# Turning the pairs' results by DMA instead of on TensorE in a two-layer macaron trunk

## The chip, the cores and the metric

The kernel runs on one core of one Trainium2 chip. The metric is the device time of one execution in microseconds (us); lower is better. The kernel before the change takes 1689.77 us, the median of three runs (1689.21 to 1690.2).

## The reference

Two layers work on a residual stream `x` of 512 tokens by 1024 features in float32. The parts that this case is about are the feed-forward networks (FFNs), two in a layer, four in all:

```
for l in range(DEPTH):                      # DEPTH = 2
    x = x + 0.5 * swiglu(rms_norm(x, ffn1_norm[l]), ffn1_wg[l], ffn1_wu[l], ffn1_wd[l])
    h = rms_norm(x, mix_norm[l])
    z = h @ w_in[l]                         # q, k, v and the three parts of a short convolution
    ...                                     # attention over a window of 128, and the convolution
    x = x + concat([attn_out, conv_out]) @ w_out[l]
    x = x + 0.5 * swiglu(rms_norm(x, ffn2_norm[l]), ffn2_wg[l], ffn2_wu[l], ffn2_wd[l])
return rms_norm(x, final_norm)

def swiglu(h, w_gate, w_up, w_down):
    return (silu(h @ w_gate) * (h @ w_up)) @ w_down     # 1024 -> 2816 -> 1024
```

## The kernel before

**Products.** Each float32 operand is split into a rounded high part and a low part, and a product is three matmuls: high by high, low by high, high by low. A weight tile is 128 partitions by 1024 elements (512 KB). SP loads it into one of eight `raw` buffers (line 188), ScalarE casts the high part into `wh` (line 204), VectorE subtracts to get `wl` (line 205), and there are three buffers of each. `take_split` hands out the next tile and asks for the split of the tile two further on (`SPLIT_AHEAD = 2`), which in turn asks for the load of a unit four further on (`LOAD_AHEAD = 4`). The order of the weight tiles is written down beforehand by `plan()` (line 376), in the same order in which the stages use them.

**Stages of an FFN.** The 2816 inner columns are 11 blocks of 256. The tuples `FIRST`, `INNER` and `LAST` (lines 32 to 40) list the stages: `p` is a plain block, `w` a pair of blocks taken together, `u` a single block, `s` a down-projection shared by two pairs, `d` a plain down-projection of the listed blocks. The first FFN of the kernel is `FIRST`, the two in the middle are `INNER`, the last one `LAST`. There are four pairs in the first FFN and five in each of the other three, 19 in all.

**A pair** is done by `winograd2` (line 1024): a seven-product scheme (`Seven`, `CHAINS`) in place of eight. Its seven steps run `stream` (line 832) twice each, 12 matmuls of 128x512 a time, so 24 matmuls a step. The results lie with tokens on the partitions. The next product needs inner columns on the partitions, so the four token blocks `ups[0..3]` of a pair have to be turned: 512 tokens by 512 columns. `turn(c)` does that with four TensorE transposes of 128x128 (line 1078) into PSUM and a ScalarE copy into `raws` (line 1082), or, for the pair of blocks 9 and 10, a split straight from PSUM. The four `turn`s of a pair wait in a list, `pending`, and are taken from it by `turns(step)` in steps 0, 1 and 2 of the next pair (one, one and two of them), or by `flush` in the second shared stage.

**Down-projection.** `share` (line 849) uses the seven-product scheme again, on two pairs at once: forms of the turned results are made by `Seven.make`, and VectorE adds the products to the stream (line 872). `down` (line 332) does the plain blocks: for each half `o` of the 1024 output columns, four PSUM banks, one for each token block; VectorE adds each to the stream (line 1150). In `INNER` and `LAST` the last stage is `("d", (0, 9, 10))`, block 0 waiting from the beginning of the FFN. In its second half (`o = 1`) three tiles are held and the first two token blocks are finished before the other two, so that the next norm can begin; `norm.pull()` puts the norm's transposes between products. In `LAST` that stage is run by `Finale` (line 1161), which also does the last norm and the stores.

**Buffers.** Turned operands, the norm's seven forms and their sums share eight buffers, tag `xf` (line 124); gates, `ups` and other 128x512 pieces share fourteen, tag `g2`; whole turned pairs (`raws`) use four, tag `g8`.

**Order.** The program is written in one order for all engines; a scheduler then sets the order on each engine by readiness and by place in the program, except in regions under `manual_schedule`, where the written order stands. Each engine and each DMA queue takes its instructions in order. SP's queue has the weight loads, POOL's queue the accumulating loads that make weight sums (line 199).

Of the kernel before, what the change touches and what calls it, by code (L numbers as in the profile page):

```python
# [10 lines left out]
BF16 = mybir.dt.bfloat16  # L11
I32 = mybir.dt.int32
AF = mybir.ActivationFunctionType
ALU = mybir.AluOpType

P = 128
D = 1024
S = 512
# [54 lines left out]
def trunk_kernel(  # L73
# [139 lines left out]
    def need_split(g):  # L213
        while state["split"] <= min(g, len(order) - 1):
            n = state["split"]
            u, what = order[n]
            far = what == "far"
            if what in (None, "wide", "far"):
                need_raw(u if far else u + LOAD_AHEAD)
# [111 lines left out]

    def down(acts, blocks, norm=None):

        last = len(blocks) - 1

        def products(acc, t, i, wh, wl):
            tok = slice(t * P, (t + 1) * P)
            ah, al = acts[blocks[i]]
            for k in range(2):
                for n, (a, w) in enumerate(((ah, wh), (al, wh), (ah, wl))):  # L340
                    nc.tensor.matmul(  # L341
                        acc,
                        a[:, k, tok],
                        w[:, k, :],
                        start=i + k + n == 0,
                        stop=i == last and k == 1 and n == 2,
                    )

        for o in range(2):
            accs = [psum("mm", [P, S], f"down_{state['group']}_{t}") for t in range(NT)]  # L350
            if o and norm:
                by_hand()
            if o and last:
                held = [take_split(SPLIT_AHEAD - i)[1:] for i in range(last + 1)]
                ahead = state["group"]
                for t in range(2):
                    for i, w in enumerate(held):
                        products(accs[t], t, i, *w)
                    yield t, o, accs[t]
                for i, w in enumerate(held):  # L360
                    for t in range(2, NT):
                        products(accs[t], t, i, *w)
                        if i == last:
                            yield t, o, accs[t]
                        if norm and i + 1 == last:
                            norm.pull()
                    need_split(ahead + i)
                continue
            for i in range(last + 1):
                _, wh, wl = take_split()  # L370
                for t in range(NT):
                    products(accs[t], t, i, wh, wl)
                    if i == last:
                        yield t, o, accs[t]

    def plan():
# [25 lines left out]
        def ffn(wg, wu, wd, stages):  # L402
            for what, b in stages:
# [13 lines left out]
                if what != "d":  # L417
                    continue
                for half in range(2):
                    for k in b:  # L420
                        u = add_unit((wd, 2 * k, 2, half * S, S))
                        if half == 0 or stages is not LAST:
                            order.append((u, "wide"))

# [461 lines left out]
    def ffn(norm, stages, whole, after=None, late=None):  # L886
# [137 lines left out]
        def winograd2(b, between=None):  # L1024
# [5 lines left out]
            ups = [None] * NT  # L1030
            kept = {}

            def keep(what, u, src):
# [3 lines left out]
            for step, (acc, operand, start) in enumerate(CHAINS):  # L1037
# [5 lines left out]
                for h in range(2):  # L1043
                    _, wh, wl = take_split()
                    stream(accs[acc], wh, wl, xh, xl, h, start)
                    for u in range(2):
# [15 lines left out]
                        if step == 5:  # L1062
                            ups[u] = kept["u2", u]
                            nc.vector.tensor_sub(ups[u], out, ups[u])
                            nc.vector.tensor_mul(ups[u], ups[u], gates[u])
                        if step == 6:
                            nc.scalar.activation(gates[2 + u], out, AF.Silu)
                            nc.vector.tensor_mul(ups[2 + u], ups[2 + u], gates[2 + u])
                turns(step)
                if between:  # L1070
                    between(step)
            if b in blocks:
                raws[b] = g8(f"raw_a_{name}", F32, (P, KC // 2, S))

            def turn(c, tag="sc"):
                tp = psum(tag, [P, S], f"at_{name}_{c}")
                for t in range(NT):
                    nc.tensor.transpose(  # L1078
                        tp[:, t * P : (t + 1) * P], ups[t][:, c * P : (c + 1) * P], ident
                    )  # L1080
                if b in raws:
                    nc.scalar.copy(raws[b][:, c, :], tp)
                    return
                if b + c // 2 not in acts:
                    acts[b + c // 2] = both(f"a_{name}_{c}", shape=(P, 2, 2, S))
                hi, lo = acts[b + c // 2]
                split(hi[:, c % 2, :], lo[:, c % 2, :], tp)

            pending.extend(lambda *tag, c=c: turn(c, *tag) for c in range(NT))

# [3 lines left out]
        def turns(step):  # L1094

            if step < 2:
                flush()
            if step == 2:
                flush(2, "mm")
# [4 lines left out]
        pending = []  # L1104

        def flush(n=1, *tag):
            for _ in range(n):
                if pending:
                    pending.pop(0)(*tag)

        for i, (what, b) in enumerate(stages):
# [11 lines left out]
            if what == "s" and b == sevens[0]:  # L1123
                then = shared(sevens[1])
                sums = ("t3", "t2") if stages[-1] == ("s", sevens[1]) else ("t2", "t3")
                share(
                    ops, 0.5, ahead(then, {3: ("b11",), 4: ("b21",), 5: sums[:1], 6: sums[1:]})
                )
            elif what == "s":
                share(  # L1130
                    then,
                    0.5,
                    None if first else lambda step: 2 <= step < 6 and flush(1, "aux"),
                    after=after if final else None,
                )
# [6 lines left out]
            if final and not after:  # L1142
# [3 lines left out]
                return  # L1146
            for n, (t, o, acc) in enumerate(down(acts, b, after if final else None)):
                if b == (0,) and first:
                    norm.make(*{0: ("t3",), 4: ("t1",)}.get(n, ()))
                nc.vector.scalar_tensor_tensor(  # L1150
                    xt(t, o), acc, 0.5, xt(t, o), op0=ALU.mult, op1=ALU.add
                )
                flush()
# [356 lines left out]
```

## Time and profile before

| | us |
|---|---|
| median of three runs | 1689.77 |
| lowest and highest | 1689.21, 1690.2 |
| the profiled execution | 1689.48 |
| its span, first to last instruction | 1687.7 |

| engine | busy us | share of the span |
|---|---|---|
| PE (TensorE matmuls) | 1674.4 | 99% |
| DVE (VectorE) | 1324.7 | 78% |
| ACT (ScalarE) | 953.4 | 56% |
| POOL (GpSimd) | 182.3 | 11% |

The mean granted TensorE clock is 0.999. The core moves 279.85 MB by DMA, 166 GB/s over the span. In the rows, names are those of tiles without their numbers: `wh` and `wl` are the high and low part of a weight tile, `x`, `y`, `w` the accumulators of a pair, `x_s`, `y_s`, `w_s` those of a shared down-projection, `at` the PSUM bank into which a pair's result is turned, `raw_a` its copy, `down` the plain down-projection. `SPq` is SP's DMA queue. An arrow after an idle time names what ended it.

### The profile page before, as it was taken

The page shows a single profiled execution, that of the slowest core. Times are in us where ns is not written, and L with a number is a line of the kernel's source. Part 1 is how long each engine was busy: PE and PEld are TensorE (multiplying, and loading weights), DVE is VectorE, ACT ScalarE, POOL GpSimd, SP SyncE. Part 2 cuts the span into 40 slices and gives each one's busy share as a digit, 9 for nine tenths or more (in the row PEclk, how much of TensorE's full clock was granted, in tenths as well). Part 3 has the DMA queues.
Part 4 walks back from the last instruction along what each step waited for, and adds up shares of the span by engine and source line. Part 5 has one row for each costly group of instructions (what it writes and reads, how often), then busy time and mean ns, then how long its engine had stood idle before and what let it go on. Part 6 is the DMA issues. An engine that isn't in the chain of part 4 may idle for free.

```text
span 1687.7 us, 21919 instructions
## 1 busy us (share of the span) xinstructions
PE 1674.4 (99%) x8222; PEld 1408.9 (83%) x8222; DVE 1324.7 (78%) x1734; ACT 953.4 (56%) x1361; POOL 182.3 (11%) x164
## 2 busy tenths in 40 slices
PE   9999999999999999999999999999999999999998
PEld 7888898888889888888898888888988898888887
DVE  7987679867799666899596668995587986678993
ACT  6445555556566555655365556554565765556553
POOL 0011111000110111111001111110001101111101
PEclk9999999999999999999999999999999999999999
DMA  8367778721495777788547776883225947777871
GB/s 250 99 176 194 184 196 209 194 72 51 125 226 124 195 181 185 187 224 214 136 100 188 187 186 176 229 219 105 59 63 151 221 119 185 188 185 185 226 188 50
DMA packets 189310, 279.85 MB, mean 166 GB/s; under 512 B 8948, under 2 KB 73492, under 8 KB 189204
## 3 DMA queue, kind: packets, MB, share of 16 engines
q1 hardware_dynamic: 150900, 203.34, 38.2%
q0 software_dynamic: 37600, 74.46, 26.1%
q8 instruction: 64, 1.05, 0.2%
q10 hardware_dynamic: 704, 0.66, 0.1%
q14 instruction: 42, 0.34, 0.1%
HBM read 263.74 MB, written 2.10 MB: 158 GB/s over the span
## 4 chain that ended last, share of the span: by engine, by line
PE 92%; DVE 6%; ACT 1%; issue 1%; DMA 0%; SPq 0%; DVEq 0%; ACTq 0%
PE x L838 25%; PE y L838 12%; PE x_s L838 10%; PE w L838 6%; PE down L341 5%; PE y_s L838 5%; PE acc L291 4%; PE acc L292 4%; PE acc L294 4%; PE w_s L838 3%; PE acc L318 2%; PE at L1078 2%; DVE wl L205 2%; PE x_m L838 1%; PE up L953 1%; PE acc L736 1%
## 5 line engine op out<-in xcount | busy, mean ns | idle before, releaser
L204 ACT CAST wh<-raw 128x1024 fp32r<-128x1024 f32 (+1 forms) x494 | 516.4, 1046 | 555.8 <-PE x L838 128.1
L205 DVE TENSOR_TENSOR wl<-raw,wh 128x1024 fp32r<-128x1024 f32 (+1 forms) x494 | 598.7, 1214 | 243.7 <-ACT wh L204 241.3
L838 PE MATMUL x<-wh,ft 128*128 128x512 f32 x608 | 188.7, 391 | 0.0
L838 PE MATMUL y<-wh,ft 128*128 128x512 f32 x608 | 188.4, 391 | 0.0
L838 PE MATMUL x<-wh,fb 128*128 128x512 f32 x608 | 187.2, 389 | 0.0
L838 PEld LDWEIGHTS x<-wh,fb 128*128 128x128 f32 x608 | 113.9, 188 | 23.5
L838 PEld LDWEIGHTS x<-wh,ft 128*128 128x128 f32 x608 | 113.1, 188 | 22.8
L838 PEld LDWEIGHTS y<-wh,ft 128*128 128x128 f32 x608 | 113.1, 188 | 22.7
L838 PE MATMUL x<-wl,ft 128*128 128x512 f32 x304 | 118.3, 389 | 0.0
L838 PE MATMUL y<-wl,ft 128*128 128x512 f32 x304 | 118.3, 389 | 0.0
L838 PE MATMUL x<-wl,fb 128*128 128x512 f32 x304 | 118.3, 389 | 0.0
L199 POOL DMA_DIRECT2D raw<-in_ffn_wu_dram x39 | 47.2, 1213 | 529.3 <-DMA raw<-in_ffn_wu_dram 272.5
L838 PE MATMUL w<-wh,fb 128*128 128x512 f32 x304 | 95.2, 394 | 0.0
L291 PE MATMUL acc<-hh,wh 128*128 128x512 f32 x240 | 94.6, 394 | 0.0
L294 PE MATMUL acc<-hh,wl 128*128 128x512 f32 x240 | 94.0, 391 | 0.0
L292 PE MATMUL acc<-hl,wh 128*128 128x512 f32 x240 | 93.6, 390 | 0.0
L341 PE MATMUL down<-wh,a 128*128 128x512 f32 x288 | 89.4, 392 | 0.0
L838 PE MATMUL y_s<-wh,ft_s 128*128 128x512 f32 x256 | 79.5, 392 | 0.0
L838 PE MATMUL x_s<-wh,ft_s 128*128 128x512 f32 x256 | 79.1, 390 | 0.0
L199 POOL DMA_DIRECT2D raw<-in_ffn_wg_dram x39 | 47.0, 1205 | 265.1 <-DMA raw<-in_ffn_wu_dram 102.0
L838 PE MATMUL x_s<-wh,fb_s 128*128 128x512 f32 x240 | 74.2, 390 | 0.0
L231 DVE TENSOR_TENSOR raw<-raw,raw 128x1024 f32<-128x1024 f32 x58 | 70.8, 1220 | 0.6
(320 smaller groups left out, 3429.1 us busy)
## 6 DMA issues: line engine op xcount, KB each, us to landing
raw<-in_ffn_wu_dram SPq DMA_DIRECT2D x126, 512.0 KB, 3.6
raw<-in_ffn_wd_dram SPq DMA_DIRECT2D x104, 512.0 KB, 4.8
raw<-in_ffn_wg_dram SPq DMA_DIRECT2D x86, 512.0 KB, 4.7
raw<-in_ffn_wu_dram POOLq DMA_DIRECT2D x39, 512.0 KB, 6.7
raw<-in_ffn_wg_dram POOLq DMA_DIRECT2D x39, 512.0 KB, 6.1
raw<-in_w_in_dram SPq DMA_DIRECT2D x36, 512.0 KB, 3.8
raw<-in_ffn_wd_dram POOLq DMA_DIRECT2D x32, 512.0 KB, 7.5
raw<-raw POOLq DMA_DIRECT2D x20, 512.0 KB, 6.6
```

Of the source, the lines that this page charges most:

```text
L199: nc.gpsimd.dma_start(out=r, in_=rows_of(*more), accum_op=ALU.add)
L204: nc.scalar.copy(hi, raw)
L205: eng.tensor_sub(lo, raw, f32(hi))
L231: nc.vector.tensor_add(a11, a11, s1)
L291: nc.tensor.matmul(acc, hi[:, k, :], rhs[k][0], start=k == first, stop=False)
L292: nc.tensor.matmul(acc, hi[:, k, :], rhs[k][1], start=False, stop=False)
L294: nc.tensor.matmul(acc, lo[:, k, :], rhs[k][0], start=False, stop=k == last)
L318: nc.tensor.matmul(accs[j][:, t * H : (t + 1) * H], w[:, k, :], x_, start=t + k + i == 0, stop=k == KC - 1 and i == 2, skip_group_check=True,)
L341: nc.tensor.matmul(acc, a[:, k, tok], w[:, k, :], start=i + k + n == 0, stop=i == last and k == 1 and n == 2,)
L736: nc.tensor.matmul(opening[n], (lo if part == "w" else hi)[:, k, :], xl if part == "x" else xh, start=n not in begun, stop=k == KC - 1 and ...
L838: nc.tensor.matmul(accs[u], x_[:, 2 * h + k, tok], w[:, k, :], start=start and h + k + i == 0, stop=h + k == 2 and i == 2, skip_group_chec ...
L1078: nc.tensor.transpose(tp[:, t * P : (t + 1) * P], ups[t][:, c * P : (c + 1) * P], ident)
```

## The change

Four things are changed.

1. `turn` goes. `apart(t)` reads each token block of a pair's result as pairs of 16-bit halves and lets ScalarE copy the low halves to one plane and the high halves to another (two copies of 128x512). `send(t)` issues one DMA transpose on SP's queue for the block's two planes, 128 partitions by 1024 halves, into its place in a tile `pt` of tag `xf`. `join(n)` lets ScalarE put the halves of two 128-column pieces together again (two copies of 128x1024) in the room of `raws`, and, for the pair of blocks 9 and 10, splits them from there.
2. When this happens is a table of steps: token blocks 0 and 1 are sent after step 0 of the next stage, 2 and 3 after step 1, and the pieces joined after steps 5 and 6. The first shared stage calls `turns` too; the second no longer does.
3. In `INNER` and `LAST`, block 0's down-projection is a stage of its own behind the first pair, so that the last `d` has blocks 9 and 10 only.
4. For the last `d` with a norm behind it there is `down_end`: all four weight tiles (two blocks by two halves) are held at once, one of them in an `xf` buffer (`"room"` in the order), and token blocks 0 and 1 are finished for both halves before 2 and 3 begin.

```diff
 INNER = (
-    ("p", 0), ("w", 1), ("w", 3), ("w", 5), ("w", 7), ("w", 9), ("s", 1), ("s", 5),
-    ("d", (0, 9, 10)),
+    ("p", 0), ("w", 1), ("d", (0,)), ("w", 3), ("w", 5), ("w", 7), ("w", 9), ("s", 1), ("s", 5),
+    ("d", (9, 10)),
 )
-LAST = INNER[:-1] + (("d", (0, 9, 10)),)
+LAST = INNER[:-1] + (("d", (9, 10)),)
...
-            hi = wpool.tile(shape, F32R, tag="wh", bufs=3, name=f"wh_{n}")
-            lo = wpool.tile(shape, F32R, tag="wl", bufs=3, name=f"wl_{n}")
+            if what == "room":
+                hi, lo = both(f"wx_{n}", shape=(P, 2, 2, S))
+            else:
+                hi = wpool.tile(shape, F32R, tag="wh", bufs=3, name=f"wh_{n}")
+                lo = wpool.tile(shape, F32R, tag="wl", bufs=3, name=f"wl_{n}")
...
+    def down_end(acts, blocks, norm):
+        a, b = blocks
+        held = []
+        def tile_of(n):
+            while len(held) <= n:
+                held.append(take_split(max(0, min(SPLIT_AHEAD, 3 - len(held))))[1:])
+            return held[n]
...
+        by_hand()
+        for t in range(2):
+            for o in range(2):
+                acc = bank(t, o)
+                for i in range(2):
+                    products(acc, t, 2 * o + i)
+                yield t, o, acc
+        ahead = state["group"]
+        for o in range(2):
+            accs = {t: bank(t, o) for t in (2, 3)}
+            for i in range(2):
+                n = 2 * o + i
+                for t in (2, 3):
+                    products(accs[t], t, n)
+                    if i:
+                        yield t, o, accs[t]
+                if n in (1, 2):
+                    norm.pull()
+                if n:
+                    need_split(ahead + n - 1)
...
+            def apart(t):
+                planes.append(g2(f"pl_{name}_{t}", U16, (P, 2, S)))
+                src = ups[t].bitcast(U16).rearrange("p (n z) -> p z n", z=2)
+                for z in range(2):
+                    nc.scalar.copy(planes[t][:, z, :], src[:, z, :])
+
+            def send(t):
+                if not turned:
+                    turned[0] = xpool.tile([P, 2 * NT, S], U16, tag="xf", bufs=8, name=f"pt_{name}")
+                nc.sync.dma_start_transpose(
+                    turned[0][:, :, t * P : (t + 1) * P], planes[t].rearrange("p z n -> p (z n)")
+                )
...
-            if b in blocks:
-                raws[b] = g8(f"raw_a_{name}", F32, (P, KC // 2, S))
-
-            def turn(c, tag="sc"):
-                tp = psum(tag, [P, S], f"at_{name}_{c}")
-                for t in range(NT):
-                    nc.tensor.transpose(
-                        tp[:, t * P : (t + 1) * P], ups[t][:, c * P : (c + 1) * P], ident
+            def join(n):
+                cs = slice(2 * n, 2 * n + 2)
+                if not n:
+                    raws[b] = g8(f"raw_a_{name}", F32, (P, KC // 2, S))
+                room = raws[b][:, cs, :]
+                apart_ = room.bitcast(U16).rearrange("p c (n z) -> p c z n", z=2)
+                for z in range(2):
+                    nc.scalar.copy(
+                        apart_[:, :, z, :], turned[0][:, NT * z + 2 * n : NT * z + 2 * n + 2, :]
                     )
-                if b in raws:
-                    nc.scalar.copy(raws[b][:, c, :], tp)
-                    return
...
+                if b not in blocks:
+                    acts[b + n] = both(f"a_{name}_{n}", shape=(P, 2, 2, S))
+                    split(*acts[b + n], room)
+
+            for step, do, ns in ((0, send, (0, 1)), (1, send, (2, 3)), (5, join, (0,)), (6, join, (1,))):
+                pending.setdefault(step, []).extend((lambda do=do, n=n: do(n)) for n in ns)
...
-            for n, (t, o, acc) in enumerate(down(acts, b, after if final else None)):
+            ends = down_end(acts, b, after) if final else down(acts, b)
+            for n, (t, o, acc) in enumerate(ends):
...
-                flush()
                 if final:
                     after(t, o)
-            if b == (0,):
+            if b == (0,) and first:
                 norm.make("t4", "b22")
```

More of the change, by code (lines that the diff above doesn't have):

```diff
@@ L12 @@
 I32 = mybir.dt.int32
+U16 = mybir.dt.uint16
 AF = mybir.ActivationFunctionType
@@ L330, in halves, with down @@
                         done(j, accs[j])
-    def down(acts, blocks, norm=None):
+    def down(acts, blocks):
         last = len(blocks) - 1
@@ L418, in ffn @@
                     continue
+                end = (what, b) == stages[-1]
                 for half in range(2):
@@ L421, in ffn @@
                         u = add_unit((wd, 2 * k, 2, half * S, S))
-                        if half == 0 or stages is not LAST:
-                            order.append((u, "wide"))
+                        if half == 0 or not end or stages is not LAST:
+                            room = end and stages is not LAST and (half, k) == (0, b[0])
+                            order.append((u, "room" if room else "wide"))
         for l in range(DEPTH):
@@ L1103, in ffn @@
         raws = {}
[L1104 to L1109, printed above, removed]
+        pending = {}
         for i, (what, b) in enumerate(stages):
```

56 lines of the change are left out of this document (24 added, 32 removed).

## The prediction

> **What bounds the kernel now.** I read the page first (busy time, slices, chain), then the chain in order of time around one pair of blocks, then busy time by stretch, then the instructions of that stretch.
>
> ```profile
> span 1687.7 us, 21919 instructions
> PE 1674.4 (99%) x8222; PEld 1408.9 (83%) x8222; DVE 1324.7 (78%) x1734; ACT 953.4 (56%) x1361; POOL 182.3 (11%) x164
> PE 92%; DVE 6%; ACT 1%; issue 1%; DMA 0%; SPq 0%; DVEq 0%; ACTq 0%
> L1078 PE MATMUL at<-ident,u x152: 270/272/273, 105.7 to 1641.9; 128*128 128x128 f32 x152
> L1078 PE MATMUL at<-ident,p x152: 272/272/328, 105.9 to 1642.1; 128*128 128x128 f32 x152
> ```
> TensorE is busy for 1674.4 of 1687.7 us and carries 92% of the chain, so time leaves the kernel only if TensorE work leaves it. The 304 transposes of pairs' results (2 x 152) are 16 for each of 19 pairs, 4 in the first FFN and 5 in each of the other three. Their 272 ns overlap, so I take their price from the chain around one pair.
>
> ```profile
> 609.18 10.88 PE x L838 x48
> 620.06 0.44 PE at L1078 x4
> 620.50 5.50 PE w L838 x24
> 626.00 0.44 PE at L1078 x4
> 626.43 5.47 PE x L838 x24
> 631.91 0.87 PE at L1078 x8
> 632.78 5.46 PE y L838 x24
> 649.12 5.89 PE x L838 x26
> ```
> Columns are start, length, what. One period of the pair loop is 649.12 - 609.18 = 39.94 us. It holds seven steps of 24 matmuls; 10.88 us for 48 makes 5.44 us a step, 38.08 us for seven. The rest, 1.86 us, is the sixteen transposes (0.44 + 0.44 + 0.87 = 1.75) and 0.11 us of slower starts behind them.
>
> ```profile
> 609.18:649.12 39.94, 39.94 (x185) 33.15 (x185) 27.79 (x28) 22.04 (x29) 4.81 (x4) 1.00 0.74 185
> 110.00:120.00 10.00, 10.00 (x48) 8.23 (x48) 9.93 (x20) 4.28 (x6) 2.41 (x2) 1.00 0.63 106
> 770.00:780.00 10.00, 10.00 (x46) 8.29 (x45) 9.74 (x11) 4.88 (x5) 3.31 (x3) 1.00 0.84 196
> 780.00:790.00 10.00, 10.00 (x47) 8.29 (x47) 10.00 (x12) 6.42 (x7) 0.86 (x1) 1.00 0.95 220
> ```
> Columns: stretch, length, busy PE, PEld, DVE, ACT, POOL, granted clock, DMA share, GB/s. In the pair loop VectorE has 12 us free, ScalarE 18, the clock is full. In the shared down-projection (770 to 790) VectorE has almost nothing free: it is next in line.
>
> **The change, part by part.**
>
> *Transposes off TensorE.* 19 x 1.86 = 35.3 us leave the chain. This is the one gain.
>
> *ScalarE.* Each pair loses four copies out of PSUM and gains eight 16-bit copies of 128x512 (apart) and four of 128x1024 (join).
> ```profile
> L1082 ACT COPY raw_a<-at 128x512 f32<-128x512 f32 x64 | 35.8, 586 | 3.1 <-PE at L1078 3.0
> L204 ACT CAST wh<-raw 128x1024 fp32r<-128x1024 f32 (+1 forms) x494 | 516.4, 1046 | 555.8 <-PE x L838 128.1
> L546 ACT ACTIVATE sq<-x 128x512 bf16<-128x512 f32 x40 | 25.1, 628 | 18.6 <-DVE x L1150 15.3 <-DVE x L872 2.9
> ```
> No row has 16-bit input with a stride. Half or double these prices are my bounds; I take them as they stand, since the nearest 16-bit row (a bf16 result, 628 ns) is no cheaper than the f32 copy (586). Per pair: 22.04 - 4 x 0.586 + 8 x 0.586 + 4 x 1.046 = 28.6 of 38.08 us (24.1 to 37.4). ScalarE's urgent work is the weight cast: a tile is cast two half-steps ahead.
> ```profile
> 614.43 1.06 ACT L204 CAST wh<-raw 128x1024 fp32r<-128x1024 f32 x1 [0.54 <-PE x L838]
> 616.89 1.22 DVE L205 TENSOR_TENSOR wl<-raw,wh 128x1024 fp32r<-128x1024 f32 x1
> 619.67 0.39 PE L838 MATMUL x<-wl,fb 128*128 128x512 f32 x1
> ```
> This tile, the tightest I found in the pair, is ready at 616.89 + 1.22 = 618.11 and wanted when the matmul row at 619.67 ends its group, at 619.9: 1.8 us to spare. A join copy in front of the cast costs at most its own 1.05 us. So zero, covered by that spare; uncovered, about 1 us a pair, 19 in all.
>
> *Four DMA transposes a pair on SP's queue, 256 KB each.* SP waits for `apart` of blocks 2 and 3, whose last product on VectorE starts at 616.29.
> ```profile
> 616.29 0.68 DVE L1068 TENSOR_TENSOR p<-p,gate 128x512 f32<-128x512 f32 x1
> 605.89 19.94 SPq L188 DMA_DIRECT2D raw<-in_ffn_wu_dram  x4
> SPq L188 <- DVE wl L205: 1194.5, 323, 21.0
> raw<-in_ffn_wu_dram SPq DMA_DIRECT2D x126, 512.0 KB, 3.6
> raw<-in_ffn_wd_dram SPq DMA_DIRECT2D x104, 512.0 KB, 4.8
> q1 hardware_dynamic: 150900, 203.34, 38.2%
> ```
> 616.29 + 0.68 + two copies (1.17) is 618.1. Behind the sends stand weight loads, and behind those POOL's accumulating loads and the casts. SP idles 1194.5 us for want of free buffers, and a load runs four tiles (10.9 us) ahead of its split against 3.6 to 4.8 us of landing: 6 us spare. Price of one transpose: the plain queue moved 203.34 MB in 0.382 x 16 x 1687.7 = 10,315 engine-us, 19.7 KB per engine-us, so 262 KB take 0.83 us of all sixteen engines; or, at 68 ns a packet (10,315 us / 150,900) and one packet for each 256-byte run of 128 halves (1,024 of them), 4.4 us. I take 0.8 to 1.2, the byte end, because most packets of that row are of kilobytes and their time goes with bytes. The loop uses 0.74 x 39.94 = 29.6 us of DMA; with 4 x 1.2 it is 34.4 of 38.08. The pair that begins at 609.18 + 5.44 = 614.6 joins them from its step 5, at 641.8, some 23 us after the last send, so nothing on TensorE waits: zero. If that cover went, the join would hold ScalarE, and the casts behind it, for what is missing.
> The Trainium skill, DMA: Bandwidth & Descriptors, section Latency and other measured facts, gives a DMA transpose 261 GB/s in one shape; my estimate by it is 1.0 us each and 33.6 us a period, no change to the sum; no run here shows it.
>
> *Summing accumulate.* The sends land among POOL's accumulating loads, whose tile is the one already late:
> ```profile
> 623.12 1.05 ACT L204 CAST wh<-raw 128x1024 fp32r<-128x1024 f32 x1 [1.24 <-issue]
> 624.21 1.23 DVE L205 TENSOR_TENSOR wl<-raw,wh 128x1024 fp32r<-128x1024 f32 x1 [1.30 <-ACT wh L204]
> ```
> It is split by 625.44 and used two half-steps after the one running, about 628.9: 3.5 us spare against two transposes of 0.8 to 1.2. Zero; at 4.4 us each it would miss by 5.
>
> *Block 9 and 10's splits earlier.* Three pairs are no longer split piece by piece in the second shared stage but by two 1.21 us subtractions inside the first one, where VectorE is full.
> ```profile
> L205 DVE TENSOR_TENSOR wl<-raw,wh 128x1024 fp32r<-128x1024 f32 (+1 forms) x494 | 598.7, 1214 | 243.7 <-ACT wh L204 241.3
> 781.66 1.05 ACT L204 CAST wh<-raw 128x1024 fp32r<-128x1024 f32 x1 [2.80 <-DVE raw L231]
> 783.21 1.22 DVE L205 TENSOR_TENSOR wl<-raw,wh 128x1024 fp32r<-128x1024 f32 x1
> 785.95 0.62 PE L838 MATMUL x_s<-wh,ft_s 128*128 128x512 f32 x2
> ```
> The tile finished at 784.43 is used at 785.95: 1.5 us spare; 2 x 1.214 = 2.4 us more ahead of it leaves TensorE 1.0 us short. I take +1.0 in each of three FFNs: +3.0 (bounds 0, if the splits slide behind urgent work, and 7.3, all of it).
>
> *Block 0's down-projection early.* Its 48 matmuls and two weight loads on SP's queue move in front of block 3's loads; none is added, and the loads' landing of 4.8 us has the same lead. It adds eight evacuations in each of three FFNs, VectorE only:
> ```profile
> L1150 DVE SCALAR_TENSOR_TENSOR x<-down,x 128x512 f32<-128x512 f32 x40 | 26.6, 686 | 13.4 <-PE down L341 13.1
> 111.92 5.49 PE down L341 x24
> ```
> 24 x 0.686 = 16.5 us, in stretches where TensorE needs two tiles instead of four. The first FFN does the same at 111.92 with VectorE at 9.93 and TensorE at 10.00 of 10 us. Zero. It frees the 8-buffer slot that the turned pieces use. Uncovered: up to 5.5 us a place.
>
> *Last two blocks' tiles held.* Same matmuls; the first two token blocks now end 48 matmuls (10.9 us) before the phase ends, formerly 36 (8.2 us), so the next norm is better covered, but four tiles must be split before the first token block is done. Its edges have shown:
> ```profile
> PE acc L318 <- DVE wl L205: 1.9, 3, 0.6
> PE up L953 <- DVE wl L205: 0.9, 3, 0.4
> PE x_m L838 <- DVE wl L205: 1.6, 2, 0.8
> ```
> I take +1.0 in all, about one more such stall at each of the two phase ends, between -0.9 (the second row's stalls vanish) and +3. In the last FFN the closing pieces only shorten from 18 matmuls to 12; the steps behind the last one stay.
>
> **Sum.** 1689.48 (this execution, 0.3 below the median of 1689.77) - 35.3 + 3.0 + 1.0 = 1658.2, so 1658.
>
> **The rivals.**
> *Part of the gain is given back.* Late casts in each pair (1 us x 19), or VectorE bound through both shared stages, which lose their 3.7 us of cover in each of four FFNs. For it: 10.00 of 10 us at 780; against: no TensorE wait inside a pair above. 1658 + 7 to 1658 + 28: 1665 to 1686.
> *ScalarE becomes the bound.* If 16-bit strided copies cost double, it needs 37.4 of 38.08 us with two waits a step, and the period stays near 39.9: 1690, no gain. Against: the rows by element above.
> *Slower: the transposes fill the DMA engines.* The place is the pair loop, the price 4.4 us each: 29.6 + 17.6 = 47.2 us a period in place of 39.94, 19 x 7.3 = 139 us more: about 1828. It decides from (39.94 - 29.6) / 4 = 2.6 us each. For it: shares of 0.84 to 0.95 in quoted stretches, small runs; against: the 23 us of patience, and the time of plain packets going with bytes.
> The Trainium skill, VectorE: DVE Perf Modes, section The three transpose paths, speaks for this rival: 1309 ns for a 128x128 16-bit block by DMA against 390 on TensorE; 32 blocks a pair one behind another would be 41.9 us by my estimate, more than a period. This trace has 272 ns for the TensorE block, 0.11 us in a row of them; no run here shows the DMA side.
>
> **How the numbers follow.** About 0.2% (3.4 us) is what a measurement can tell from none. Forecast (1652 to 1664) 0.56; part given back 0.24; ScalarE bound, within 0.2%, 0.04; slower by DMA, or by some wait of ScalarE on a late transfer, 0.16. Faster 0.80, same 0.04, slower 0.16. The range 1652 to 1686 takes the first two. Its low end is 1689.5 - 35.3 - 0.9 - 1.6, the last two being the stalls of the `up` and `x_m` rows.
>
> **What would show it.** Right: no `at` group; 7,918 matmuls; pair periods of 38.1 us; ScalarE near 28.6 us in each; transposes landed before 625 of a like pair; short VectorE waits of TensorE in the first shared stage only. Wrong: periods at 40 or more with DMA share at 1.0, casts waiting on DMA, or joins waiting on the turned tile.

## The result, and the profile after

The changed kernel takes 1738.57 us (median, 1733.19 to 1748.13) against 1689.49 us for the kernel before beside it: ratio 1.0296, 95% interval 1.0242 to 1.035. It is 3% slower; 1658 us was forecast, in a range of 1652 to 1686. The profiled execution took 1733.68 us, 44.2 us more than that of before. First the page of the changed kernel: span, busy times, the chain by engine, the queue that carries the weights and now the transposes (packets, MB, share of the time of 16 DMA engines), and the row of the join copies.

```profile
span 1731.9 us, 21677 instructions
PE 1661.6 (96%) x7912; PEld 1380.8 (80%) x7912; DVE 1335.5 (77%) x1752; ACT 1076.3 (62%) x1519; POOL 182.4 (11%) x164
PE 61%; DVE 9%; ACT 6%; DMA 6%; issue 3%; ACTq 0%; DVEq 0%
q1 hardware_dynamic: 231156, 223.27, 45.5%
L1135 ACT COPY raw_a<-pt 128x1024 uint16<-128x1024 uint16 x76 | 101.4, 1352 | 109.4 <-DMA pt<-pl 89.3 <-issue 20.2
```

TensorE has 310 matmul records fewer, yet it carries 61% of the chain in place of 92%, and stands still for 70 us (1731.9 - 1661.6) in place of 13. The last row has the new wait: before its 76 join copies ScalarE was idle for 109.4 us, 89.3 of them put down to the turned tile. The view of waits (total, times, longest) has who paid:

```profile
ACT raw_a L1135 <- DMA pt<-pl: 89.3, 16, 11.5
PE y_s L874 <- ACT wh L205: 25.0, 3, 9.1
PE x L874 <- ACT wh L205: 14.0, 7, 4.4
```

TensorE waits for casts of weights (`wh`), not for the turned results. One place in the timeline of the changed kernel shows the link (start, length, engine, what, idle time before it): SP's queue, then ScalarE's, then TensorE.

```profile
626.85 10.86 SPq L1081 DMA_TRANSPOSE pt<-pl  x4
...
635.12 1.05 ACT L205 CAST wh<-raw 128x1024 fp32r<-128x1024 f32 x1
636.07 0.58 ACT L1087 COPY p<-x 128x512 f32<-128x512 f32 x1
645.47 1.33 ACT L1135 COPY raw_a<-pt 128x1024 uint16<-128x1024 uint16 x1 [8.82 <-DMA pt<-pl]
646.67 1.03 ACT L205 CAST wh<-raw 128x1024 fp32r<-128x1024 f32 x1
...
647.75 1.22 PE L874 MATMUL x<-wh,ft 128*128 128x512 f32 x2 [4.39 <-ACT wh L205]
```

The four sends take SP from 626.85 to 637.71. The first join stands on ScalarE's queue right behind the two `p` copies of step 0 of the next pair, not among the copies of step 5, where the code writes it. ScalarE reaches it at 636.65, while SP still has the fourth send. It waits 8.82 us there; behind it stands a cast of a weight tile, and TensorE is out of work for 4.39 us. The stop has a second price: the busy time by stretch (stretch, length, busy PE, PEld, DVE, ACT, POOL, granted clock, DMA share, GB/s) shows the granted clock go down with it.

```profile
632.00:640.00 8.00, 8.00 (x37) 6.63 (x36) 6.78 (x7) 4.46 (x7) 0.97 (x1) 1.00 1.40 127
640.00:650.00 10.00, 5.57 (x19) 3.77 (x18) 1.84 (x3) 4.53 (x5) 0.00 (x0) 0.78 0.68 117
754.70:764.70 10.00, 10.00 (x45) 8.26 (x45) 9.76 (x12) 10.00 (x15) 4.23 (x4) 1.00 1.20 207
764.70:774.70 10.00, 6.52 (x29) 5.07 (x27) 4.31 (x5) 0.28 (x1) 0.00 (x0) 1.00 1.11 216
774.70:784.70 10.00, 4.35 (x9) 2.98 (x10) 3.68 (x4) 7.62 (x8) 0.00 (x0) 0.53 0.62 187
```

Two matmuls took 1.22 us behind the stop, 0.61 to 0.62 us elsewhere. The last two rows lie in the first shared stage: a join holds ScalarE for 12.10 us (the profile puts this wait down to "issue"; the fourth transpose of that pair landed at 777.01, the join began at 777.08), and TensorE's clock falls to 0.53. The Trainium skill, TensorE: Matmul & The Clock Gate, section Why this matters for your kernels, asks for no idle gap above some 3 us between bursts of matmuls, since the clock is halved behind one; this trace agrees, with 1.22 us behind a gap of 4.39 us.

For the rest of this part I read the length of each stage from the matmul records, from its first matmul to the first of the next stage. "Pairs" is w1 to w9 of a later FFN without block 0's down-projection, "shared" s1 and s5, three values for the three FFNs; "first FFN" is its second down-projection, its pairs and block 10, and s2. All in us; the kernel before took 1689.5 to 1690.1 us beside each of them. The stages are those of the profiled execution, whose time stands beside the median: that of e1_hold was the fastest of its ten, so its median is 7.7 us above what its stages show.

| kernel | median | profiled | first FFN | pairs | shared |
|---|---|---|---|---|---|
| before | 1689.5 | 1689.5 | 190.9 | 197.9 (each) | 78.1 (each) |
| changed | 1738.6 | 1733.7 | 196.9 | 201.8, 202.8, 197.1 | 89.1, 87.4, 88.5 |
| e12_unheld | 1699.3 | 1701.6 | 192.8 | 191.8, 192.6, 193.7 | 86.0, 87.7, 86.6 |
| e1_hold | 1696.4 | 1688.7 | 191.2 | 191.1 (each) | 81.2, 85.8, 86.9 |
| e5_gain | 1693.0 | 1688.7 | 191.5 | 191.1 (each) | 80.0, 89.3, 84.0 |
| e6_late | 1686.1 | 1688.6 | 191.4 | 191.1 (each) | 83.3, 85.2, 85.0 |
| e8_soon | 1678.6 | 1679.7 | 193.9 | 190.4 (each) | 81.5, 80.9, 81.5 |
| e3_plain | 1672.4 | 1671.6 | 188.1 | 191.1 (each) | 80.0 (each) |
| e7_mix | 1668.4 | 1669.9 | 189.9 | 191.1 (each) | 78.1 (each) |
| e10_best | 1666.1 | 1666.0 | 187.2 | 191.1 (each) | 78.1 (each) |
| e11_best_soon | 1663.1 | 1663.1 | 187.0 | 190.4 (each) | 78.1 (each) |

The changed kernel loses 6.0 us in the first FFN, 8.0 in the pairs and 30.7 in the shared stages, 44.7 together; its span grew by 44.2.

### The profile page after: what moved, and what is told of

The parts are those of the page before. It is cut to its first block, busy times and chain, and to the rows that moved or that the text cites. A ratio compares the mean times of both kernels' runs of the same rounds, so it can differ in the third digit from the quotient of the medians.

```text
span 1731.9 us, 21677 instructions
## 1 busy us (share of the span) xinstructions
PE 1661.6 (96%) x7912; PEld 1380.8 (80%) x7912; DVE 1335.5 (77%) x1752; ACT 1076.3 (62%) x1519; POOL 182.4 (11%) x164
## 3 DMA queue, kind: packets, MB, share of 16 engines
q1 hardware_dynamic: 231156, 223.27, 45.5%
## 4 chain that ended last, share of the span: by engine, by line
PE 61%; DVE 9%; ACT 6%; DMA 6%; issue 3%; ACTq 0%; DVEq 0%
PE x L874 14%; PE y L874 8%; PE x_s L874 7%; DMA pt<-pl 6%; PE y_s L874 6%; DVE wl L206 3%; PE acc L295 3%; PE acc L298 3%; PE acc L296 3%; PE down L378 3%; PE down L345 3%; PE acc L322 2%; ACT wh L205 2%; PE w L874 2%; PE x_m L874 2%
## 5 line engine op out<-in xcount | busy, mean ns | idle before, releaser
L205 ACT CAST wh<-raw 128x1024 fp32r<-128x1024 f32 (+1 forms) x493 | 513.0, 1044 | 372.6 <-PE y L874 69.8
L874 PE MATMUL x<-wh,ft 128*128 128x512 f32 x608 | 191.1, 396 | 14.4 <-ACT wh L205 14.0
L1135 ACT COPY raw_a<-pt 128x1024 uint16<-128x1024 uint16 x76 | 101.4, 1352 | 109.4 <-DMA pt<-pl 89.3
L874 PE MATMUL y_s<-wh,ft_s 128*128 128x512 f32 x256 | 84.1, 411 | 25.0 <-ACT wh L205 25.0
L874 PEld LDWEIGHTS y_s<-wh,ft_s 128*128 128x128 f32 x256 | 51.0, 201 | 36.9 <-ACT wh L205 26.3
L874 PEld LDWEIGHTS x<-wl,ft 128*128 128x128 f32 x304 | 57.8, 190 | 25.0 <-DVE wl L206 13.4
```

The lines of the kernel that those rows point to most:

```text
L205: nc.scalar.copy(hi, raw)
L874: nc.tensor.matmul(accs[u], x_[:, 2 * h + k, tok], w[:, k, :], start=start and h + k + i == 0, stop=h + k == 2 and i == 2, skip_group_chec ...
L1135: nc.scalar.copy(apart_[:, :, z, :], turned[0][:, NT * z + 2 * n : NT * z + 2 * n + 2, :])
```

## The experiments

### Holding the joins back

Theory: the joins' place on ScalarE's queue makes the loss. Rival: transposes load the DMA engines, wherever the joins stand.

```diff
-            else:
-                split(hi, lo, raw)
+            else:
+                state["cast"] = split(hi, lo, raw)      # split returns its cast
...
             for do in pending.pop(step, ()):
-                do()
+                with tc.issue_after(state["cast"]) if step >= 5 else nullcontext():
+                    do()
```

> The changed kernel with one thing more: the two joins of a pair are queued on ScalarE behind the weight cast of the step at which the source calls them (5 and 6); nothing is left out. Theory A (in the changed kernel the joins stand on ScalarE's queue in the first step of the next pair, wait there for the last transpose, and hold the weight casts behind them): the waits on the turned tile (89 us) and most of TensorE's waits on casts go, the time falls from 1738 to about 1660 (1652 to 1675). Rival B (the transposes fill the DMA engines, and the weight loads come late whatever ScalarE does): casts now wait on loads, 1700 or more. Rival C (ScalarE is too full in steps 5 and 6 with 1.35 us join copies): 1675 to 1700, casts behind joins and apart copies.

1696.4 us (1688.73 to 1709.13), ratio to before 1.004 (1.002 to 1.0061): 42 us of the loss are gone. In the profile no join waits for `pt` any more and the pairs take 191.1 us, 6.8 less than before. So the place of the joins was a cause, as theory A has it, but its 1652 to 1675 us were not reached. The time lies in rival C's range, with B's sign: casts wait 28.4 us for weight loads. What remains is in the shared stages and in the first FFN. In each of the three later shared stages SP stands behind the fourth transpose of the last pair, for 11.53, 12.94 and 14.20 us, and a weight tile comes late. First the timeline of SP in the third of them, with ScalarE's largest wait; then the rows of the turned tile: time of one transpose on SP in ns, and time to landing in us, min/median/max each; then the busy time by stretch.

```profile
1571.26 7.03 SPq L1082 DMA_TRANSPOSE pt<-pl  x3
1578.39 2.88 SPq L1267 DMA_DIRECT2D gain<-in_final_norm_dram  x2
1581.36 14.20 SPq L1082 DMA_TRANSPOSE pt<-pl  x1
1595.66 10.32 SPq L189 DMA_DIRECT2D raw<-in_ffn_wd_dram  x8
...
1601.51 1.04 ACT L205 CAST wh<-raw 128x1024 fp32r<-128x1024 f32 x1 [10.41 <-DMA raw<-in_ffn_wd_dram]
```
```profile
L1082 SPq DMA_TRANSPOSE pt<-pl x76: 1237/1482/14199, 101.6 to 1581.4; - x76
DMA to landing us min/median/max: 3.1/4.9/19.0
```
```profile
1581.00:1595.50 14.50, 14.50 (x65) 12.01 (x64) 13.46 (x15) 7.33 (x8) 0.00 (x0) 1.00 1.45 97
1595.50:1605.00 9.50, 5.25 (x18) 3.52 (x17) 1.87 (x2) 2.77 (x3) 0.00 (x0) 0.77 0.98 281
```

The weight loads at 1595.66 stood behind the fourth transpose for 14.20 us, and the cast of the first of them waited 10.41 us. The hold is not SP's alone: while it lasts the DMA share is 1.45 (the times of all packets are added up, so it can pass 1) and yet only 97 GB/s move, against 281 behind it. The second gain load, a plain DMA issued just before the transpose, took 19.1 us to land. POOL's two sums from SBUF to SBUF, issued at 1576.68 and 1579.14, took 18.9 and 19.6 us, where they took 8.6 and 8.9 in e3_plain (below), which has plain DMAs in place of the transposes. So here the transposes slow the DMAs that are in flight beside them.

### The other parts of the change alone

Block 0's down-projection early and the last two blocks' tiles held, with the turns left on TensorE as before (`down`, `down_end` and the `room` tile of the change too; its pairs, joins and sends are not in it).

```diff
 INNER = (
-    ("p", 0), ("w", 1), ("w", 3), ..., ("s", 5), ("d", (0, 9, 10)),
+    ("p", 0), ("w", 1), ("d", (0,)), ("w", 3), ..., ("s", 5), ("d", (9, 10)),
 )
```

> The kernel before with the two other parts alone: block 0's down-projection early and the last two blocks' four tiles held; pairs are still turned on TensorE. Theory A and rival B both put the loss on the transposes: 1688 to 1692. Rival D (the moved stages themselves open gaps at their edges, 3 us waits at the early down-projection): 1694 or more.

1690.1 us, ratio 1.000 (0.999 to 1.0009). These parts alone neither cost nor give anything that can be measured. The loss comes with the DMA transposes and the copies around them.

### Plain DMAs of the same bytes

```diff
-                nc.sync.dma_start_transpose(
-                    turned[0][:, :, t * P : (t + 1) * P], planes[t].rearrange("p z n -> p (z n)")
-                )
+                nc.sync.dma_start(
+                    turned[0][:, :, t * P : (t + 1) * P],
+                    planes[t].rearrange("p z (c n) -> p (z c) n", n=P),
+                )
```

On e1_hold (e3_plain) and on the changed kernel itself (e12_unheld).

> e1_hold with each DMA transpose replaced by a plain DMA of the same 256 KB between the same tiles in runs of 256 bytes; the results of pairs are not turned, that part of the computation is left out. Theory A: what remains after the hold isn't the crossbar, so within 5 us of e1_hold. Rival B with the crossbar as the cause: at least 10 us below e1_hold, and loads land sooner. If small runs are the price, the same time as e1_hold and the same number of packets.

> The changed kernel with the plain DMA of e3_plain in place of the transpose, its joins not held back, so that they stand where the changed kernel has them on ScalarE's queue; the turning is left out, so the output is not the reference's. Theory (the place of the joins costs most of the loss, with any DMA that takes some 6 us to land): pair stages are again 6 to 11 us longer than the 153.0 us of e3_plain, and the run takes 1690 to 1715 us. Rival (the loss of the changed kernel is that transposes are slow, and its joins would have found plain DMAs landed): within 5 us of e3_plain, 1672 to 1677 us.

e3_plain: 1672.42 us, ratio 0.9898 (0.9882 to 0.9915). e12_unheld: 1699.3 us, ratio 1.0056 (1.0041 to 1.0071). The four medians make a square:

| | joins where the queue had them | joins held |
|---|---|---|
| DMA transpose | 1738.6 | 1696.4 |
| plain DMA | 1699.3 | 1672.4 |

The place of the joins costs 42.2 us with transposes and 26.9 with plain DMAs; the transpose costs 39.3 us over a plain DMA with the joins early, 24.0 with the joins held. So neither theory alone has the loss: place and transfer are both in it, and 15.3 us are there only where both meet. Theory A of e3_plain (within 5 us of e1_hold) failed; rival B's 10 us or more came, with nearly as many packets on the queue (229,940 against 231,156), so the number of small packets is not what the 24.0 us pay for. The expectation of e12_unheld had the total right and the stages wrong: the pairs lost 0.7 to 2.6 us against e3_plain, not 6 to 11, and the shared stages 6.0 to 7.7. (In e12_unheld the join also stands one cast later on ScalarE's queue at the place shown above, so that column is not the same queue to the instruction.)

SP tells the two kinds of DMA apart, in this row of e3_plain beside the same two of e1_hold above; the median time to landing is not longer for the transposes (4.9 us against 6.2), the longest is (19.0 against 12.2):

```profile
L1082 SPq DMA_DIRECT2D pt<-pl x76: 593/789/4635, 101.6 to 1569.6; - x76
DMA to landing us min/median/max: 2.9/6.2/12.2
```

e3_plain still lies 14 us above the forecast, and its shared stages show most of it. Busy time by stretch, of e3_plain, then of before:

```profile
765.60:775.60 10.00, 9.84 (x44) 7.82 (x43) 8.35 (x9) 9.88 (x10) 1.04 (x2) 1.00 0.97 216
775.60:785.60 10.00, 9.36 (x42) 7.39 (x41) 10.00 (x11) 4.59 (x6) 2.05 (x2) 1.00 0.70 118
785.60:795.60 10.00, 8.18 (x35) 6.15 (x34) 10.00 (x11) 7.14 (x8) 1.76 (x2) 1.00 0.78 164
```
```profile
764.30:774.30 10.00, 10.00 (x46) 8.29 (x45) 9.74 (x11) 5.19 (x5) 1.08 (x1) 1.00 0.94 252
774.30:784.30 10.00, 10.00 (x46) 8.29 (x45) 10.00 (x11) 4.74 (x5) 3.09 (x4) 1.00 1.00 175
784.30:794.30 10.00, 10.00 (x48) 8.26 (x47) 9.54 (x12) 5.02 (x6) 0.00 (x0) 1.00 0.85 255
```

The last pair's joins come in steps 5 and 6 of the shared stage, ScalarE is full there (9.88 of 10), VectorE's sums and splits pile up behind it (10.00 twice), and TensorE goes hungry. The stage has lost the last pair's turns, worth 1.86 us in a pair stage, and is still 1.9 us longer. No run parts the joins on ScalarE from the splits on VectorE.

### One transpose, alone and beside other DMAs

Two kernels that leave out the model and have little but DMAs. The first has four transposes one at a time, then four at once, then eight 512 KB loads alone, then both mixed (on SP's queue the mixed part stood as three transposes, eight loads and the last transpose):

```diff
+    for n in range(8):
+        load(8 + n)
+        if n % 2:
+            turn(more, n // 2, mid[1])        # a DMA transpose of SP
```

> Only DMA: four transposes of 128x1024 16-bit, each waiting for the one before; four back to back; eight 512 KB weight loads; eight loads with a transpose behind every second. All of the model is left out. Theory A: alone, one lands in about 3 us, the least seen in the changed kernel (3.1), four back to back in about 4 x 1.9 us plus that, so the 6.1 us median there is queueing behind loads and each other. Rival E (the transpose is slow by itself): 6 us alone.

Median times to landing in its view of DMAs (one at a time is `one`, four at once `many`, mixed `more`), then two rows of SP's timeline:

```profile
many<-mid SPq DMA_TRANSPOSE x4, 3.3
more<-mid SPq DMA_TRANSPOSE x4, 5.7
one<-mid SPq DMA_TRANSPOSE x3, 3.1
```
```profile
18.76 5.37 SPq L96 DMA_TRANSPOSE many<-mid  x4
45.76 5.30 SPq L96 DMA_TRANSPOSE more<-mid  x1
```

Alone one lands in 3.1 us, as theory A has it. Four at once hold SP for 5.37 us together and have all landed 7.2 us after the first was issued, sooner than its 4 x 1.9 + 3; one that follows eight loads holds SP for 5.30 us by itself and lands after 10.1 us. The second kernel asks what makes it so. Its edit, for stretch (b):

```diff
+        for i in range(2):
+            nc.gpsimd.dma_start(out=raw[i], in_=raw[2 + i], accum_op=ALU.add)
+        ...                                   # VectorE writes src, some 2.5 us
+        for t in range(2):
+            nc.sync.dma_start_transpose(to[:, :, t, :], src)
```

> No part of the model is computed; six stretches one after the other, each with two DMAs on SP's queue: DMA transposes (a) alone, (b) some 4 us behind two accumulating 512 KB DMAs of POOL from SBUF into SBUF, (c) behind two accumulating 512 KB loads of POOL from HBM, (d) behind the two gain loads; then a plain copy of the same 256 KB (e) alone and (f) behind two accumulating DMAs as in (b). Theory (a transpose queued behind POOL's SBUF accumulates holds SP until they are through): in (b) a transpose holds SP for 5 us or more and lands 8 us or later, while (a), (c) and (d) hold 1.2 to 2 us and the plain copy of (f) holds under 2 us. Rival (only the number of packets in flight matters): (b) and (c), which move the same bytes, hold SP alike.

```profile
L130 SPq DMA_TRANSPOSE to<-src x2: 1322/1324/1327, 45.4 to 46.8; - x2
L130 SPq DMA_TRANSPOSE to<-src x2: 1739/3086/4432, 53.6 to 55.4; - x2
L130 SPq DMA_TRANSPOSE to<-src x2: 1445/2816/4187, 65.5 to 67.0; - x2
L130 SPq DMA_TRANSPOSE to<-src x2: 1243/1284/1325, 76.8 to 78.1; - x2
L128 SPq DMA_DIRECT2D to<-src x2: 667/678/688, 84.9 to 85.6; - x2
L128 SPq DMA_DIRECT2D to<-src x2: 594/666/739, 92.7 to 93.3; - x2
```

The rows are the stretches (a) to (f) in order; numbers are ns min/median/max on SP. Behind two of POOL's DMAs a transpose holds SP for up to 4.43 us, whether they go from SBUF to SBUF (b) or come from HBM (c): the rival has it, not the SBUF accumulate, and the theory's 5 us of hold and 8 us to landing were not reached. Behind the gain loads (d) it holds no longer than alone. A plain copy beside the same accumulates (f) holds SP for 0.74 us. Landing was alike: 6.3 to 6.9 us in (b) and (c), 6.0 to 6.5 in (f). So beside this traffic a transpose is hardly slower to land than a copy; it keeps the queue, and with it what stands behind. The Trainium skill, Advanced Engine Details and Errata, section X-Bar Transpose (TRN2), says that transpose DMAs are as fast as regular ones; the landing times agree, the 24.0 us between e1_hold and e3_plain and the two holds on SP do not. The holds of 11.53 to 14.20 us in e1_hold are more than these two kernels reached; in stretch (b) POOL's sums still landed after 5.3 and 7.7 us, so why all DMAs get so slow in the model stays open.

### Which place in the model

Four edits on e1_hold: the gain loads queued behind the weight loads of the second shared stage (e5_gain); the last pair's joins moved to the second shared stage (e6_late); the last pair of each FFN turned on TensorE (e7_mix); all joins two steps earlier (e8_soon).

```diff
# e5_gain, at both places that load a gain
+                with tc.issue_after(state["load"]):     # the last weight load traced
                     nc.sync.dma_start(...)
# e6_late
+                if do is join and b not in blocks:
+                    room, step = later, step - 3        # run by the second shared stage
# e7_mix
+            by_dma = b < 8                              # else the turns of before, at their places
# e8_soon
-            ..., (5, join, (0,)), (6, join, (1,))):
+            ..., (3, join, (0,)), (4, join, (1,))):
```

> e1_hold with one thing moved: the two gain loads (a row of 512 broadcast to 128 partitions, 256 KB each), which stand on SP's queue between the third and the fourth DMA transpose of the last pair, are queued behind the weight loads of the second shared stage. Theory (gain loads beside transposes): the fourth transpose no longer holds SP for 14.2 us, the weight tiles behind it are on time, the three shared stages fall from 81.3, 85.9 and 87.1 us to the 80.1 that the plain DMA had, and the run takes about 1682 us. Rival (the transposes are slow beside the weight loads whatever else runs): SP is still held over 10 us and the run stays at 1694 to 1698 us.

> e1_hold with the joins and splits of the last pair (blocks 9 and 10) moved from steps 5 and 6 of the first shared stage to steps 2 and 3 of the second, where the TensorE turns of the kernel before stood. Theory (VectorE bunching: in the run with plain DMA it was busy 10.00 of 10 us in two slices of the first shared stage while TensorE fell to 8.2 to 9.4 of 10): some 3 us a layer of INNER come back, 1696.4 - 10 = about 1686 us. Rival (VectorE's work is the same wherever it stands, or the late weight tiles decide alone): no change, 1694 to 1698 us.

> e1_hold with the last pair of every stage list (w9, and w8 in FIRST) turned on TensorE at the places of the kernel before; the other 15 pairs go by held DMA transposes. Theory (loss sits only where transposes meet a shared stage or its gain loads): the pair stages keep their gain, 12 x 1.62 us in INNER and 3 x 1.6 us in FIRST, and the rest is as before: 1689.5 - 24 = about 1665 us. Rival (the extra packets slow the weight loads everywhere): 1675 us or more.

> e1_hold with every join at steps 3 and 4 in place of 5 and 6, still behind the last cast before it. Theory (late joins bunch VectorE's work at the end of the step that follows; landing median 4.9 us is early enough): the shared stages lose their idle TensorE time, 1680 to 1688 us. Rival (the wait for a turned tile comes back, since a transpose of step 1 lands up to 19.0 us after its issue and step 3 comes some 11 us after it): joins wait for pt again and the run takes over 1700 us.

e5_gain: 1693.0 us, ratio 1.0018 (1.0002 to 1.0034), with shared stages of 253.3 us together against 253.9. SP is still held for up to 11.68 us. The rival's case: the gain loads are not it, as (d) above also says.

e6_late: 1686.12 us, ratio 0.9968 (0.9947 to 0.9988), as the theory had it, but its mechanism is only half shown: TensorE's wait in `w_s` for VectorE fell from 3.6 to 1.6 us and its wait in `x_s` for a cast from 3.6 to 0.9, while late weight tiles took 15.9 us in `y_s` in place of 10.1, so the profiled execution (1688.6 us) is no shorter than that of e1_hold (1688.7).

e7_mix: 1668.43 us, ratio 0.9872 (0.9856 to 0.9887). Fifteen pairs still go by DMA; the shared stages are back at 78.1 us, the pairs stay at 191.1. Nearly all of the loss that the held joins leave sits where transposes meet the shared stages.

e8_soon: 1678.6 us, ratio 0.9937 (0.9917 to 0.9957), just below the theory's 1680 to 1688. The rival's waits came back in part (9.5 us in four places), but the shared stages are shorter and the longest hold of SP is 3.87 us. Here, in the three later FFNs, the last pair's fourth transpose was issued 5.3 to 5.8 us behind the start of POOL's last summing DMA, in e1_hold 0.5 to 2.2 us behind it. That this shortened the hold fits e9_beside and was not tried alone.

### A version that beats both

From e7_mix: the first pair of the first FFN, whose transposes ran inside a down-projection (15.2 us there, 10.9 with plain DMAs), turned on TensorE too; then the joins two steps earlier.

```diff
-            by_dma = b < 8
+            by_dma = b < 8 and not (first and b == 2)
# e11_best_soon only: joins at steps 3 and 4, held from step 3 on
```

> e7_mix with the first pair of FIRST (w2) turned on TensorE too, in steps 0 to 2 of the pair after it: 14 of 19 pairs go by held DMA transposes, none of them sent in a down-projection or in a shared stage. Theory (what is left of the loss in e7_mix is the 15.2 us down-projection of FIRST, 10.9 us where its DMAs were plain): that stage falls to 10.9 us, w4 pays 1.6 us for the turns: 1668.4 - 4.3 + 1.6 = about 1665.7 us. Rival (the stage waits for a weight tile whatever w2 does): 1669 to 1670 us.

> e10_best with the joins of the 14 pairs at steps 3 and 4 in place of 5 and 6, each behind the last cast before it. Theory (a held join is free in a pair stage wherever its tile has landed): within 1 us of e10_best a layer, 1662 to 1668 us. Rival (a transpose that lands over 8 us after its issue holds ScalarE again at step 3): 1675 us or more.

1666.08 us, ratio 0.9859 (0.9842 to 0.9875), and 1663.1 us, ratio 0.9841 (0.9826 to 0.9856): the second is 27 us below the 1690.05 us of before in the same runs. The page of the second, then its rows of the turned tile:

```profile
span 1661.3 us, 21763 instructions
PE 93%; DVE 5%; ACT 1%; issue 0%; DMA 0%; SPq 0%; DVEq 0%; ACTq 0%
L1139 ACT COPY raw_a<-pt 128x1024 uint16<-128x1024 uint16 x56 | 74.0, 1354 | 0.0
```
```profile
L1083 SPq DMA_TRANSPOSE pt<-pl x56: 1243/1501/3884, 152.4 to 1521.2; - x56
DMA to landing us min/median/max: 3.1/5.2/8.7
```

The joins wait for nothing, TensorE is back at 93% of the chain, and no transpose takes over 8.7 us to land.

## Why the prediction was wrong

**The step that failed** is the zero for the four transposes, in its sentence that a pair "joins them from its step 5, at 641.8, some 23 us after the last send, so nothing on TensorE waits: zero". I took the step at which the code writes the join for its place on ScalarE's queue. The queue is ordered by when work is planned to be ready: the join stood in the next pair's first two steps, with no cover at all. The sentence behind it, that without that cover "the join would hold ScalarE, and the casts behind it", is what the rows at 645.47 and 647.75 show. It was filed under the slower rival, at 0.16, as a wait of ScalarE on a late transfer. The 23 us of cover were none: ScalarE reached the first join at 636.65, before SP was done with the sends at 637.71. Price: 42.2 us (changed kernel to e1_hold).

**The transposes' own price** failed in kind and in size. Engine time of the queue: 0.455 x 16 x 1731.9 = 12,608 engine-us against 10,315 before; 2,293 more for 76 transposes are 30.2 each, 1.9 us of all sixteen engines, where I took 0.8 to 1.2. Most of that is not the transposing: the plain DMAs of e3_plain come to 23.5 each by the same sum (a share of 45.3% of a span of 1669.8 us), and alone, in stretch (a) of e9_beside, two transposes took 56.0% of 5 us, 22.4 each. It stayed under the 2.6 at which the rival decided, and no pair stage was DMA-bound: the pairs take 191.1 us with transposes (e1_hold) and with plain DMAs (e3_plain). The 1,056 packets each ((231,156 - 150,900) / 76) were about the 1,024 guessed, the 4.4 us each did not come. What I left out was SP: "behind the sends stand weight loads", and I priced the loads' 6 us of spare but not the queue, held for up to 14.20 us by one transpose while the DMAs beside it slowed down. Price: 24.0 us by the medians of e1_hold and e3_plain; the profiled executions have 17.1 of it, 13.9 in the shared stages and 3.1 in the first FFN, none in the pairs. The Trainium skill's price in VectorE: DVE Perf Modes, section The three transpose paths, 41.9 us a pair by my estimate, did not come either: four transposes, 32 such blocks, have landed 7.2 us after the first was issued in e4_alone.

**Block 9 and 10's splits** were mis-sized: +3.0 us. Their mechanism, VectorE full in the first shared stage, was right as far as it went: in e3_plain ScalarE waits 17.1 us there for VectorE (`ACT ft_s L205 <- DVE raw_a L676`). But ScalarE is full there too, which I had looked at in the pairs alone. With the DMAs made plain, the shared stages of the three FFNs are 1.89 us longer each where 1.86 us of turns left them: 11.2 us, for joins and splits together. The first FFN, where I had put nothing, adds the 3.9 us by which its s2 grew (38.1 to 42.0).

**Transposes off TensorE** were right. In e11_best_soon four pairs' turns leave the stage: (197.87 - 190.43) / 4 = 1.86 us a pair, as forecast.

**ScalarE's copies** were a little dearer, 1.352 us for a join where 1.046 was taken and 0.62 where 0.586 was, and cost nothing in the pairs of e11_best_soon, where no join waited. That rival (1690) had the wrong mechanism.

**The early down-projection and the held tiles**, 0 and +1.0: e2_orders has them at ratio 1.000 (0.999 to 1.0009).

The signs named for "wrong" were the ones seen: joins waiting on the turned tile, and DMA share above 1.0 beside them. The ones for "right" that came: no `at` group, and 7,912 matmul records where 7,918 were named.

## What to carry to other kernels

A copy that waits for a DMA makes everything behind it wait on its engine's queue, so its price is read from its place on that queue, not from its line in the code; tie it behind an instruction that comes late enough (42.2 us here). When a DMA is added to a queue that also issues loads, count how long it keeps the queue beside other traffic, and keep it out of the stages where the next load has no spare. Taking 1.86 us from TensorE paid here in stages where the engines and the queue that take over the work have room, 14 of the 19 pairs.

## What the runs showed of the hardware that was not expected

- A DMA transpose of 256 KB keeps SP for 1.24 to 1.33 us alone, up to 4.43 us behind 1 MB of POOL's DMAs and 5.30 us behind eight weight loads; a plain copy kept it 0.59 to 0.74 us alone and beside POOL's DMAs. In the model the longest holds were 14.20 us (e1_hold) and 4.63 us (e3_plain).
- Landing is alike for both: 3.1 to 3.4 us alone, 6.0 to 6.9 us beside those DMAs of POOL.
- In e1_hold, while one transpose held SP for 14.20 us, the core moved 97 GB/s by DMA, against 281 GB/s right behind it, and POOL's sums in flight took 18.9 and 19.6 us to land in place of the 8.6 and 8.9 of e3_plain.
- A 16-bit copy of 128x1024 on ScalarE takes 1.352 us where its output has a stride of two; in e4_alone a 16-bit copy of that size between contiguous runs took 1.044 us.
- Where TensorE had stood still for 4.39 us, two matmuls took 1.22 us in place of 0.62, and the granted clock of the 10 us was 0.78.
